# A two-layer trunk kernel: the second layer's first four tiles in pairs, features outermost, with a software-pipelined norm

## The chip, the cores and the metric

The kernel runs on one core of a Trainium2 chip. The metric is the device time of one execution in microseconds (us); lower is better. The engines named below are PE (TensorE, matmuls), DVE (VectorE), ACT (ScalarE), POOL (GpSimd) and SP (SyncE, which issues the DMAs). Each engine takes its instructions in the order in which the program was written for it; semaphores hold an instruction until its inputs are there.

## What is computed

Two layers of a trunk with four parallel branches, for 128 context tokens and 512 latent tokens (640 columns in all), with a model width of 1024. Cut to what matters here:

```python
def trunk_layer(x, cond, lp, ctx=None):
    mod = jax.nn.silu(cond) @ lp['w_mod'] + lp['b_mod']
    shift, scale, gate = jnp.split(mod[:, None, :], 3, axis=-1)
    h = rmsnorm(x, lp['g_norm']) * (1 + scale) + shift
    (a_u, a_v, b_r, b_k, b_v, b_wd, b_ad, c_q, c_k, c_v, d_p, z, mg) = split_in(h @ lp['w_in'])
    y_a = chunk_mix(a_u, a_v, ...)
    y_c = attention(c_q, c_k, c_v, ...)
    y_b, s_fin = rwkv7_mix(b_r, b_k, b_v, b_wd, b_ad, ...)
    y_d = pool_mix(d_p, ...)
    ys = jnp.stack([y_a, y_b, y_c, y_d], axis=2) * jax.nn.silu(z)
    up = jnp.einsum('blnc,ncd->blnd', ys, lp['w_up'])
    merged = jnp.sum(jax.nn.sigmoid(mg) * up, axis=2)
    return x + gate * (merged @ lp['w_o'])
```

The product `h @ w_in` is made tile by tile of 128 output columns. Its first four tiles are the keys, the values and the two query tiles of the attention: c_k, c_v, and two halves of c_q.

## The kernel before

**Layout.** Activations lie with features on the 128 partitions: the width of 1024 is eight blocks of features (`KT` = 8), and the 640 tokens are two halves `b` of 320 columns (`hs`, `segs`). The first half holds all context tokens, which have a modulation of their own, so a normed feature has two segments there and one in the second half.

**Products.** Every float32 product is made of three passes in a reduced format. Weight and activation are each split into a high and a low part, and `accum` (line 450) issues, for each feature block, hi x hi, hi x lo and lo x hi into one PSUM tile. The weights come in pieces of half a tile (four feature blocks). `piece()` hands out the next one in the order of the list `pieces`, and `split` makes the high part on ACT (`whi`) and the low part on DVE (`wlo`), by default two pieces ahead. `whi` and `wlo` have three buffers each, so a piece's buffers come free when the piece three before it has been used. The four PSUM tiles `m` take the products of the tiles, and `evac` copies them out on ACT and DVE in turn.

**The norm.** `normed` (line 603) takes the sum of squares through a matmul, a square root on ACT and a reciprocal on DVE. Then for each feature block: `t` = x times the modulation's scale times the norm's factor on DVE, `hi` = t + shift on ACT (rounded to the reduced format), and `lo` = t + shift - hi on DVE. With `ahead` set, `lo` of a block is issued behind `t` of the next one; without it, right after `hi`. In the first layer both halves go through it together with `ahead`; in the second layer each half has a call of its own, as soon as the last layer's output projection of that half is done, with `ahead` = 0.

**The order of work.** A planner in the kernel (class `Clock`) runs while the program is written. The main line is a generator whose matmuls fill PE; side jobs (norms, modulation, attention, scan, pooling) are generators too, and the planner steps each of them when, by its own reckoning, its inputs are ready. `yield VQ` lets a job rest until DVE's queue is nearly empty. What comes out is a fixed order of instructions for each engine.

**The head of the second layer.** `head` (line 1276) makes the tiles `HEAD` = ck, cv, q0, q1 for the first half of tokens while the second half's norm runs, and then for the second half. Each tile takes its eight feature blocks one after the other, waits for block k of the norm (`yield f"h{l}{b}.{k}"`), and is copied out by `put`, which marks the tile as ready after the second half. The weights of these tiles lie in SBUF already (`resident`, filled by `hold_wo`) and are split anew for each half of tokens. `attention` waits for the norm, then for ck, cv and q0, and rotates the keys and queries (`rotate`: a shuffle, two products, one of them on POOL, and a sum). q1 is rotated by a job of its own. Scores, softmax and values then run as side jobs. After the head the main line makes nine more tiles (wa, k0, v0, r0, k1, r1, v1, and the two gates z20 and z21), and `gated(None, ...)` needs the attention's result before it goes on. The scan of the second branch runs beside all this.

Of the kernel before, what the change touches and what calls it, by code (L numbers as in the profile page):

```python
# [17 lines left out]
KT = D // P  # L18
# [7 lines left out]
PASSES = (2, 0, 3, 1)  # L26

HEAD = ["ck", "cv", "q0", "q1"]
ORDER = ["wa", "k0", "v0", "r0", "k1", "r1", "v1", "z20", "z21", "p0", "av0", "p1", "av1", "au0", "au1", 0,
         "z00", "z01", 1, "z30", "z31", 2, "z10", "z11", 3]  # L30
A_TILES = HEAD + [n for n in ORDER if isinstance(n, str)]
A_INDEX = {n: i for i, n in enumerate(A_TILES)}
# [262 lines left out]
def hybrid_layers_kernel(ctx: ExitStack, tc: tile.TileContext, xt, cond, condb, wm, wt, wa, wb, wo, pa, pb, pc, gfin, kctx, vctx,  # L295
# [10 lines left out]
    def S(shape, tag, bufs=1, dt=F32):  # L306
        return ck.alloc(tag, sb.tile(shape, dt, tag=tag, name=tag, bufs=bufs), bufs)

    def M():
        return ck.alloc("m", ps_m.tile([P, HF], F32, tag="m", name="m"), 4)  # L310
# [10 lines left out]
    ck = Clock()  # L321
    V, A, G, PE = Engine(nc.vector, "V", ck), Engine(nc.scalar, "A", ck), Engine(nc.gpsimd, "G", ck), nc.tensor

    def dma(out, in_, wait=False, scale=4):
        ck.dma(out, in_, scale * out.size(), wait)
        nc.sync.dma_start(out, in_)
# [42 lines left out]
    pieces = []  # L369
    for l in range(NL):  # L370
        def a_piece(n, h):
            pieces.append((wa[l, A_INDEX[n]][:, 4 * P * h:4 * P * h + 4 * P], 4))

        if l == 0:
            for group in (HEAD[0:3], HEAD[3:4]):
                for h in range(2):
                    for n in group:
                        a_piece(n, h)
        else:
            for n in HEAD * 2:  # L380
                for h in range(2):
                    pieces.append(((l, n, h), 4))
        for it in ORDER:
            if isinstance(it, int):
                for d in range(KT):
                    for h in range(2):
                        pieces.append((wb[l, it, d][:, 5 * P * h:5 * P * h + 5 * P], 5))
            else:
                for h in range(2):
                    a_piece(it, h)  # L390
        for b in range(2):
            for d in range(KT):
                for h in range(2):
                    pieces.append(((l, d, h), 4))
    raws, splits, resident, x_first = {}, {}, {}, {}
    nxt = [0, 0, 0]
# [47 lines left out]
    def piece(ahead=2):  # L444
        i = nxt[2]
        nxt[2] += 1
        split(i + ahead)
        return splits.pop(i)
# [193 lines left out]
    def ksl(tl):  # L642
        return lambda k: tl[:, k]
# [8 lines left out]
    def layer(l, h, prb):  # L652
        rhs_h = []
# [622 lines left out]
        def head():  # L1276
            inputs["cv"] = S([P, T], "bon")
            at = None

            def put(n, b, o):  # L1280
                nonlocal at
                if at is None:
                    at = S([P, 2560], "xm0")
                    inputs["ck"] = at[:, 0:T]
                    inputs["kc"] = at[:, T:T + 256]
                    dma(inputs["kc"], kctx[l])
                    for f in range(2):
                        inputs[f"q{f}"] = at[:, T * (f + 1) + 256:T * (f + 2) + 256]
                evac(target(n, b), o)
                if b:  # L1290
                    ck.mark(L + n)

            ck.spawn(f"{L}at", attention(), 0)
            if l == 0:
                for b in range(2):
                    yield f"hh{l}{b}"
                rhs_h.extend((ksl(h[b][0]), ksl(h[b][1])) for b in range(2))
                out = [[M(), M()], [M(), M()], [CB()[:, 0:HF], OB()[:, 0:HF]]]
                ws = [piece(2 - i) for i in range(3)]
                for k in range(KT):  # L1300
                    turn = k % 4 == 3
                    for b, i in [(b, i) for i in range(3) for b in range(2)] if turn else [
                            (b, i) for b in range(2) for i in range(3)]:
                        yield f"h{l}{b}.{k}"
                        yield from accum([out[i][b]], ws[i], k % 4, 1, [rhs_h[b]], k, k == 0, k == KT - 1)
                        if turn and b:
                            if k + 1 < KT:
                                ws[i] = piece(0)
                            else:
                                split(nxt[2] + i)  # L1310
                yield f"n{l}0"
                for i in range(3):
                    for b in range(2):
                        put(HEAD[i], b, out[i][b])
                o = yield from main()
                for b in range(2):
                    put(HEAD[3], b, o[b])
            else:
                for b in range(2):
                    yield f"hh{l}{b}"  # L1320
                    rhs_h.append((ksl(h[b][0]), ksl(h[b][1])))
                    for n in HEAD:
                        o = M()
                        for hf in range(2):
                            w = piece()
                            for k in range(4):
                                yield f"h{l}{b}.{4 * hf + k}"
                                yield from accum([o], w, k, 1, [rhs_h[b]], 4 * hf + k, hf == 0 and k == 0,
                                                 hf == 1 and k == 3)
                        yield f"n{l}0"  # L1330
                        put(n, b, o)
        def scans(ta, k0, v0, kx):
            yield f"{L}atp"
            yield f"{L}wa"
            yield from scan(0, ta, k0, ta[:, 2], v0)
            yield from scan(1, S([P, 4, T], "A0"), kx[:, 0], kx[:, 1], kx[:, 2])
# [89 lines left out]
    def program():  # L1426
        xs, accs = [], []
        pbs = [S([P, NPB], "pb")]

        def x_half(b):  # L1430
            xh = x_tile(b)
            for k in range(0, KT, 4):
                dma(xh[:, k:k + 4], xt[:, b, k:k + 4])
            xs.append(xh)

        def params():
            dma(c_sb[:, CST_1:], cst[:, CST_1:])
            dma(pbs[0], pb[0])
            dma(gf, gfin)

        x_half(0)
        x_half(1)
        mod_tiles(0)
        mod = modulation([(0, n) for n in range(KT)], {1: lambda: load(2), KT: params})
        next(mod)
        for b in range(2):
            acc = S([P, HF], "nacc", 2)
            if b == 0:
                for k in range(KT):
                    sq_add(acc, xs[b][:, k], k == 0)  # L1450
            else:
                odd = S([P, 2, T], "yb")[:, 0, 0:HF]
                for k in range(KT):
                    sq_add(odd if k % 2 else acc, xs[b][:, k], k < 2, G if k % 2 else V)
                V.tensor_tensor(acc, acc, odd, ALU.add)
            accs.append(acc)
        for b in range(2):
            rstd_of(accs[b])
        split(1)
        end, ck.end = ck.end, ck.t  # L1460
        ck.spawn("mods0", mod, 0, ("x", 1))
        ck.end = end
        h = {}
        ck.spawn("n00", normed(xs, accs, 0, h, range(2), 1), 0, None)
        ck.spawn("rows", modulation_rows(), 3, None)
        for l in range(NL):
            if l:
                pbs.append(S([P, NPB], "pb"))
                dma(pbs[l], pb[l])
            mhl, sm = yield from layer(l, h, pbs[l])  # L1470
            h, xs = {}, []
            for b in range(2):
                acc = S([P, HF], "nacc", 2)
                xh, sq = yield from out_proj(l, b, mhl, acc, sm, xs)
                if l + 1 < NL:
                    dma(x_next[l][:, b], xh)
                    ck.spawn(f"n{l + 1}{b}", normed({b: xh}, {b: acc}, l + 1, h, [b], 0, sq), 0, None)
                else:
                    def fin(xh=xh, acc=acc, sq=sq, b=b):
                        rs = rstd_of(acc, sq)  # L1480
                        A.activation(xh[:, KT - 1], xh[:, KT - 1], AF.Copy, scale=gf[:, KT - 1:KT])
                        yield
                        for k in range(KT):
                            E = G if k in (1, 3, 6) else V
                            E.tensor_tensor(xh[:, k], xh[:, k], rs, ALU.mult)
                            if k % 2:
                                dma(y_o[:, b, k - 1:k + 1], xh[:, k - 1:k + 1])
                    ck.spawn(f"f{b}", fin(), 0)

    ck.run(program())  # L1490


# [132 lines left out]
```

## Time and profile before

| | us |
|---|---|
| median of 3 runs | 1424.76 |
| lowest and highest | 1424.6 to 1425.26 |
| the profiled execution | 1419.62 |
| its span on the core | 1417.8 |
| PE matmuls busy | 1355.5 (96%) |
| DVE busy | 946.1 (67%) |
| ACT busy | 567.3 (40%) |
| mean granted clock of PE | 0.988 |

Times inside the program count from the start of the span. A row of a timeline gives the start, the duration, the engine, the line of the code and the operation, what it writes and what it reads, and, in brackets, how long the engine had been idle before it and what released it. Most work goes through helpers, so the line is that of a helper (L289 for DVE and ACT, L330 for matmuls), and the tiles' names tell what it is. [...]

### The profile page before, as it was taken

The page shows a single profiled execution, that of the slowest core. Times are in us where ns is not written, and L with a number is a line of the kernel's source. Part 1 is how long each engine was busy: PE and PEld are TensorE (multiplying, and loading weights), DVE is VectorE, ACT ScalarE, POOL GpSimd, SP SyncE. Part 2 cuts the span into 40 slices and gives each one's busy share as a digit, 9 for nine tenths or more (in the row PEclk, how much of TensorE's full clock was granted, in tenths as well). Part 3 has the DMA queues.
Part 4 walks back from the last instruction along what each step waited for, and adds up shares of the span by engine and source line. Part 5 has one row for each costly group of instructions (what it writes and reads, how often), then busy time and mean ns, then how long its engine had stood idle before and what let it go on. Part 6 is the DMA issues. An engine that isn't in the chain of part 4 may idle for free.

```text
span 1417.8 us, 27575 instructions
## 1 busy us (share of the span) xinstructions
PE 1355.5 (96%) x11274; PEld 1254.9 (89%) x11274; DVE 946.1 (67%) x2096; ACT 567.3 (40%) x1252; POOL 50.1 (4%) x43
## 2 busy tenths in 40 slices
PE   5899989999999999999989998999999999999996
PEld 3788878988999989999979887898899999899996
DVE  7667678755777757558886667795466585464476
ACT  5455622235522333325444554223445233233363
POOL 0100000000000000000001000000000000000011
PEclk9999999999999999999999999999999999999998
DMA  9411114421223422751213111423112323134011
GB/s 372 144 53 61 68 48 116 118 70 55 81 79 103 120 71 66 241 203 63 74 61 114 58 56 50 116 74 103 40 54 70 93 80 87 39 131 169 28 38 74
DMA packets 86502, 132.59 MB, mean 94 GB/s; under 512 B 44744, under 2 KB 46152, under 8 KB 84456
## 3 DMA queue, kind: packets, MB, share of 16 engines
q1 hardware_dynamic: 86376, 130.84, 29.1%
q8 instruction: 88, 1.44, 0.4%
q14 instruction: 38, 0.31, 0.1%
HBM read 120.46 MB, written 10.35 MB: 92 GB/s over the span
## 4 chain that ended last, share of the span: by engine, by line
PE 84%; DVE 9%; ACT 4%; issue 2%; DMA 1%; SPq 0%; DVEq 0%; ACTq 0%
PE m L330 67%; PE x L330 9%; PE c L330 4%; PE o L330 2%; DVE wlo L289 2%; DVE t L289 2%; PE x L334 1%; DVE nacc L289 1%; DVE kb L289 1%; DVE lo L289 1%; ACT A L289 1%; PE o L334 1%; ACT vn L289 1%; DVE xm L289 1%; ACT whi L289 1%
## 5 line engine op out<-in xcount | busy, mean ns | idle before, releaser
L330 PE MATMUL m<-hi,whi 128*128 128x320 f32 x2064 | 668.4, 324 | 5.5 <-ACT hi L289 3.6
L330 PE MATMUL m<-lo,whi 128*128 128x320 f32 x2064 | 641.9, 311 | 4.6 <-DVE lo L289 3.8
L330 PE MATMUL m<-hi,wlo 128*128 128x320 f32 x2064 | 641.8, 311 | 2.5 <-DVE wlo L289 2.5
L330 PEld LDWEIGHTS m<-hi,whi 128*128 128x128 f32 x2064 | 391.0, 189 | 31.2 <-issue 12.0
L330 PEld LDWEIGHTS m<-lo,whi 128*128 128x128 f32 x2064 | 391.1, 189 | 9.6 <-DVE lo L289 6.1
L330 PEld LDWEIGHTS m<-hi,wlo 128*128 128x128 f32 x2064 | 390.6, 189 | 5.7 <-DVE wlo L289 5.4
L289 ACT CAST whi<-raw 128x640 fp32r<-128x640 f32 (+1 forms) x220 | 148.5, 681 | 282.1 <-PE m L330 264.2
L289 DVE TENSOR_TENSOR wlo<-raw,whi 128x640 fp32r<-128x640 f32 (+1 forms) x220 | 167.7, 765 | 112.8 <-ACT whi L289 110.4
L289 ACT ACTIVATE t<-m 128x320 f32<-128x320 f32 x160 | 68.0, 436 | 87.6 <-PE m L330 87.5
L289 DVE SCALAR_TENSOR_TENSOR t<-t,m 128x320 f32<-128x320 f32 x128 | 61.6, 481 | 57.9 <-PE m L330 42.8
L289 DVE TENSOR_TENSOR kb<-kb 80x31 f32<-80x31 f32 (+15 forms) x248 | 88.7, 358 | 12.5 <-DMA kb<-ad 5.7
L330 PE MATMUL m<-ysh,whi 128*128 128x320 f32 x256 | 83.5, 326 | 1.8 <-DVE t L289 1.6
L289 DVE CUSTOM_DVE_ANT_0 junk<-wt,sil 128x1024 bf16<-128x1024 f32 x64 | 78.1, 1220 | 4.9 <-DMA wt<-wt 4.8
L330 PE MATMUL m<-ysh,wlo 128*128 128x320 f32 x256 | 79.1, 309 | 0.0
L330 PE MATMUL m<-ysl,whi 128*128 128x320 f32 x256 | 79.0, 309 | 0.0
L330 PEld LDWEIGHTS m<-ysh,whi 128*128 128x128 f32 x256 | 48.0, 188 | 5.1 <-DVE t L289 2.1
L289 DVE TENSOR_TENSOR xm<-xm,t 128x320 f32<-128x320 f32 x96 | 48.5, 506 | 3.3
L289 DVE RECIPROCAL t<-t 128x320 f32<-128x320 f32 x16 | 34.4, 2149 | 21.3 <-ACT t L289 21.3
L330 PEld LDWEIGHTS m<-ysl,whi 128*128 128x128 f32 x256 | 48.1, 188 | 0.4
L330 PEld LDWEIGHTS m<-ysh,wlo 128*128 128x128 f32 x256 | 48.1, 188 | 0.0
L289 ACT ACTIVATE vn<-c 64x128 f32<-64x128 f32 x40 | 10.8, 271 | 80.8 <-DVE vn L289 80.8
L289 DVE CUSTOM_DVE_ANT_0 kbt<-x,xm 128x256 f32<-128x256 f32 (+2 forms) x72 | 28.6, 434 | 14.8 <-PE x L330 14.7
(234 smaller groups left out, 1519.6 us busy)
## 6 DMA issues: line engine op xcount, KB each, us to landing
raw<-wb SPq DMA_DIRECT2D x128, 320.0 KB, 2.8
raw<-wa SPq DMA_DIRECT2D x92, 256.0 KB, 2.7
wt<-wt SPq DMA_DIRECT2D x32, 512.0 KB, 3.7
A<-wm SPq DMA_DIRECT2D x4, 1024.0 KB, 9.0
A<-wo SPq DMA_DIRECT2D x8, 512.0 KB, 3.7
xm<-xt SPq DMA_DIRECT2D x4, 640.0 KB
ad<-A SPq DMA_DIRECT2D x8, 320.0 KB, 3.8
qr<-wm SPq DMA_DIRECT2D x2, 1024.0 KB
```

Source lines behind the costliest of these rows:

```text
L289: return f(out, *a, **k)
L330: PE.matmul(out, lhsT, rhs, start=start, stop=stop)
L334: PE.transpose(out, in_, K("ident"))
```

## The change

In the second layer, the second half of tokens is walked in two pairs of tiles, ck with cv and q0 with q1 (`PAIRS`). Within a pair the feature blocks are outermost: block k of the norm is multiplied into both tiles before block k+1 is waited for. The list of pieces follows: for this half it goes pair by pair, first halves of both tiles, then second halves. Three pieces are split at the start of each half pair, and the fourth when the first tile of the pair is through with its first half. The first half of tokens is walked as before. The norm of the second half is called with `ahead` = 1 (`b` takes the place of 0), that of the first half stays as it was.

```diff
@@ pieces
         else:
-            for n in HEAD * 2:
+            for n in HEAD:
                 for h in range(2):
                     pieces.append(((l, n, h), 4))
+            for pair in PAIRS:
+                for h in range(2):
+                    for n in pair:
+                        pieces.append(((l, n, h), 4))
@@ head
                 for b in range(2):
                     yield f"hh{l}{b}"
                     rhs_h.append((ksl(h[b][0]), ksl(h[b][1])))
+                    if b:
+                        break
                     for n in HEAD:
...
+                for pair in PAIRS:
+                    out = [M(), M()]
+                    for k in range(KT):
+                        if k % 4 == 0:
+                            ws = [piece(2), piece(1)]
+                        yield f"h{l}1.{k}"
+                        for i in range(2):
+                            yield from accum([out[i]], ws[i], k % 4, 1, [rhs_h[1]], k, k == 0, k == KT - 1)
+                            if k % 4 == 3 and i == 0:
+                                split(nxt[2] + 1)
+                    for i, n in enumerate(pair):
+                        put(n, 1, out[i])
@@ program
-                    ck.spawn(f"n{l + 1}{b}", normed({b: xh}, {b: acc}, l + 1, h, [b], 0, sq), 0, None)
+                    ck.spawn(f"n{l + 1}{b}", normed({b: xh}, {b: acc}, l + 1, h, [b], b, sq), 0, None)
```

## Rows read from the trace of the kernel before

**Rows 1.** Windows of the head: stretch, length, each engine's busy time, clock, DMA.

```profile
737.60:746.70 9.10, 5.38 (x14) 3.06 (x14) 6.58 (x13) 2.75 (x5) 0.00 (x0) 0.71 0.08 26
746.70:758.40 11.70, 11.70 (x78) 11.69 (x78) 7.86 (x17) 5.02 (x10) 1.66 (x1) 0.93 0.46 158
```

**Rows 2.** Timeline of PE over the head: start, duration, operation, idle time before.

```profile
739.82 0.42 PE L330 MATMUL m<-hi,whi 128*128 128x320 f32 x1 [2.09 <-ACT hi L289]
...
748.27 0.31 PE L330 MATMUL m<-hi,whi 128*128 128x320 f32 x1
...
758.36 0.31 PE L330 MATMUL m<-hi,wlo 128*128 128x320 f32 x1
```

**Rows 3.** Timeline of DVE over the second half's norm.

```profile
727.38 0.55 DVE L289 SCALAR_TENSOR_TENSOR lo<-t,shift,hi 128x320 fp32r<-128x320 f32 x1 [0.63 <-ACT hi L289]
728.21 1.29 DVE L289 TENSOR_TENSOR wlo<-kx,whi 128x512 fp32r<-128x512 f32 x2 [0.28 <-ACT whi L289]
729.42 0.48 DVE L289 COPY bon<-m 128x320 f32<-128x320 f32 x1
729.82 0.68 DVE L289 TENSOR_TENSOR wlo<-vn,whi 128x512 fp32r<-128x512 f32 x1
...
743.73 0.55 DVE L289 SCALAR_TENSOR_TENSOR lo<-t,shift,hi 128x320 fp32r<-128x320 f32 x1 [0.63 <-ACT hi L289]
744.20 0.55 DVE L289 SCALAR_TENSOR_TENSOR t<-xm,gsc,nacc 128x320 f32<-128x320 f32 x1
745.38 0.55 DVE L289 SCALAR_TENSOR_TENSOR lo<-t,shift,hi 128x320 fp32r<-128x320 f32 x1 [0.63 <-ACT hi L289]
```

**Rows 4.** Timeline of ACT over the head.

```profile
726.78 0.56 ACT L289 ACTIVATE hi<-t,shift 128x320 fp32r<-128x320 f32 x1 [2.81 <-DVE t L289]
727.25 0.41 ACT L289 COPY xm<-m 128x320 f32<-128x320 f32 x1
727.55 1.14 ACT L289 CAST whi<-kx 128x512 fp32r<-128x512 f32 x2
...
754.63 0.43 ACT L289 COPY xm<-m 128x320 f32<-128x320 f32 x1 [1.29 <-PE m L330]
```

**Rows 5.** Timeline of PE around the wait for the attention.

```profile
866.92 0.31 PE L330 MATMUL m<-hi,wlo 128*128 128x320 f32 x1
...
873.84 1.85 PE L330 MATMUL x<-bon,cst 128*128 128x320 f32 x4 [3.42 <-DVE bon L289]
```

**Rows 6.** Timeline of ACT: the attention's last copy.

```profile
870.47 0.27 ACT L289 COPY y<-o 128x128 f32<-128x128 f32 x1 [1.43 <-PE o L330]
```

**Rows 7.** Timeline of DVE: the rotations and first scores, and the first gated product.

```profile
758.31 0.73 DVE L289 STREAM_SHUFFLE vn<-xm 128x512 f32<-128x512 f32 x1
...
760.96 0.69 DVE L289 TENSOR_TENSOR xm<-xm,vn 128x512 f32<-128x512 f32 x1 [1.19 <-POOL xm L289]
...
761.64 0.48 DVE L289 COPY xm<-m 128x320 f32<-128x320 f32 x1
...
764.00 0.28 DVE L289 CUSTOM_DVE_ANT_0 kbt<-x,xm 128x128 f32<-128x128 f32 x1
...
765.43 0.73 DVE L289 STREAM_SHUFFLE vn<-xm 128x512 f32<-128x512 f32 x1
...
873.70 0.48 DVE L289 SCALAR_TENSOR_TENSOR t<-t,m 128x320 f32<-128x320 f32 x1
```

**Rows 8.** Windows of PE alone: length, busy time, clock, DMA share, GB/s.

```profile
22.00:24.00 2.00, 1.10 (x16) 1.00 1.02 341
...
872.00:874.00 2.00, 0.16 (x1) 1.00 0.12 28
874.00:876.00 2.00, 2.00 (x6) 0.63 0.00 0
```

**Rows 9.** Windows of PE in both layers, without heads and tails.

```profile
70.00:690.00 620.00, 607.45 (x5176) 0.99 0.30 94
760.00:1340.00 580.00, 569.91 (x4926) 0.99 0.27 79
```

More of the change, by code (lines that the diff above doesn't have):

```diff
@@ L28 @@
 HEAD = ["ck", "cv", "q0", "q1"]
+PAIRS = (HEAD[0:2], HEAD[2:4])
 ORDER = ["wa", "k0", "v0", "r0", "k1", "r1", "v1", "z20", "z21", "p0", "av0", "p1", "av1", "au0", "au1", 0,
```

## Prediction

> **What bounds the kernel now.** I read the page's busy shares first: the matmul engine (PE) is busy nearly all the time, so the change can pay only where PE stands still, or where its clock is low. The change touches one place, the first four tiles of the second layer (ck, cv, q0, q1; "the head" below), so I read that stretch alone: the windows, then the timelines of PE, VectorE (DVE) and ScalarE (ACT) beside each other. In 9.1 us from 737.6 PE is busy 5.4 us at a mean clock of 0.71, and the next stretch still has 0.93 [rows 1]. PE has walked the first four features of ck for the second half of the tokens and then waits 2.09 us for the next feature's hi part [rows 2]. This norm is therefore what ends last: its last lo starts at 745.38 and ends at 745.93 [rows 3]. From there PE runs without a gap to the last matmul of q1 at 758.36 [rows 2].
>
> Why the norm is slow is seen on DVE: of each feature it computes t, then waits 0.63 us for ACT's hi, then computes lo [rows 3]. Where nothing else is queued between, a feature costs 1.65 us (from the lo at 743.73 to the one at 745.38): twice 0.47 of DVE's time, and 0.7 of waiting and handing over.
>
> The third place to look is where the head's work ends up. The tiles feed the attention, which runs beside the main line, and the main line needs its result before the first gated product. The last matmul of the main line before that point starts at 866.92 [rows 5]. The attention's last copy is at 870.47 [rows 6]. The first step of the gated product on DVE follows at 873.70 [rows 7], because the scan's work stands ahead of it there; PE had waited 3.42 us up to 873.84 [rows 5]. So the main line arrives some 3 us early at this point: a head that is shorter for the main line alone only waits longer there.
>
> **The change, part by part.**
>
> *Pipelined norm.* On DVE, feature k's lo moves behind feature k+1's t. The count of instructions stays: 8 t, 8 hi, 8 lo. The wait of 0.63 us is filled by a lo, which takes 0.47 of it. But eight weight halves are also split in this stretch: ACT casts the high part (whi), DVE subtracts it (wlo). ACT takes its queue in order: in the rows, the casts of two halves at 727.55 stand behind the hi of 726.78, which had itself waited 2.81 us for t [rows 4]. With the lo moved, t of the next feature is queued earlier, and its hi stands in front of the next cast. Then wlo can start only 1.71 us after the start of t: 0.58 to hi (t's 0.55 and a handover), 0.47 from hi to what stands behind it (726.78 to 727.25), and 0.66 from a cast to its wlo (727.55 to 728.21) [rows 3, 4]. Of these DVE fills 0.47 with t and 0.47 with one lo; 0.77 is left as a wait. [...]
>
> Bounds: if DVE never waited after its first t, 16 norm steps at 0.47, nine wlo at 0.60 (two from 728.21 to 729.42) and two copies at 0.40 [rows 3] make 13.7 us, and from the first t at 726.2 (0.58 ahead of its hi) the norm would end at 739.9, 6 us earlier. With 0.77 us ahead of six of the wlo, 4.6 in all, and 1.5 us ahead of the first (from 726.7 to 728.21, with no lo to fill it) it ends at 746.0. I take the second, no gain, since each of these waits follows from the queue's order: a feature with a split behind it cost 1.65 + 0.60 = 2.25 us before, and costs 0.47 + 0.47 + 0.77 + 0.60 = 2.3 after; the last three features, which had no split between them, get three. The other end stays for the range.
>
> *Features outermost in pairs.* The same 96 matmuls per half of tokens run; two tiles now take each feature when it comes. At 745.93 the old order has 74 matmuls left. The new one has at most 9 of the pair ck/cv (the last feature and what waits of the one before) and 48 of q0/q1, 57 in all. One step is 0.147 us (65 steps from 748.27 to 758.36, less 0.5 for five transposes among them) [rows 2]. The old rest took 758.5 - 745.93 = 12.6 us: 10.9 of steps, 0.5 of transposes, and about 1.2 for the first eight at the lower clock (the window to 758.4 has 0.93 [rows 1]).
>
> *A tighter split.* The three buffers of split weights now serve two tiles at once, so the fourth half of a pair is cast only when the first tile has left its first half, 6 matmuls (0.88 us) before it is needed; before, a half was split two halves (24 matmuls) ahead. Cast to end of wlo takes 728.21 - 727.55 + 0.68 = 1.34 us [rows 3, 4]. That is a new wait of about 0.5 us at each half, of which the norm hides the one inside ck/cv; two remain, 1.0 us. If a rotation (3.3 us on DVE, from the shuffle at 758.31 to the end of the sum at 761.65 [rows 7]) comes ahead of such a wlo, the wait is up to 3 us more; I take none, since the halves are asked for before the marks that release a rotation.
>
> New rest: 57 x 0.147 + 0.5 + 1.0 = 9.9 us, so the head ends at 755.8 instead of 758.5: **2.7 us** for the main line. SP's queue: the weights of the head lie in SBUF, and the first load of wa still goes out three pieces ahead of its split, now at the end of ck/cv; that is half a pair (24 steps, 3.5 us) before the split and a whole one before its use. I cost the DMAs at nothing; without that cover a late load would hold wa by as much as it is late. POOL has nothing here but its product in each rotation, which moves with it.
>
> *What the attention gets.* Tile ck is finished at the same time as before, for it ends with the norm. cv is ready 4 us earlier, and is not what the attention waits for last. q0, copied at 754.63 before [rows 4], is now ready with q1 at the end of the head, about 755.8 to 756.2. Its rotation on DVE started at 758.31, 3.7 us after the copy; the same delay would make it 1.2 us later, no delay 2.1 us earlier. q1's copy was at 761.64 and its rotation at 765.43, between the first block's scores (764.00) and the rest of that block [rows 7]; it can now follow q0's at 759.6, up to 5.8 us earlier. The ends are therefore +1.2 and -5.8; I take **-2**, the bound of q0, on which the first scores wait.
>
> **How it sums.** At the wait near 867 the later of two counts: the main line arrives 2.7 us earlier, the attention 2 us earlier, so 2.0 us remain. After that point PE is bound by its own matmuls. In the profiled run (1419.62, of which the span is 1417.8) this makes 1417.6; the median of the runs shown is 5.14 above that execution, and moves likewise: 1424.76 - 2.0 = **1422.8**.
>
> **The rivals.**
> 1. *The attention does not follow.* Its start keeps the 3.7 us after the copy, or the shared wait at 867 swallows all: gain 0 to 1, 1424.2. For it: the norm and ck end when they did. A version of it is the clock: six matmuls (0.88 us) per feature of 2.3 us keep PE 40% busy over the end of the norm. PE fell to the lower clock after a stretch of 0.16 in 2 us (872 to 874), and kept the full one at 1.10 in 2 us [rows 8], so this lies between. A fall costs about 1.2 us, as now, which leaves 1.5 of the 2.7 for the main line. Chance 0.20 in all. [...]
> 2. *More is given back.* The norm ends earlier, between 739.9 and 745.9, and q1's early rotation takes 3.3 us out of the attention's first blocks: 4 to 7 us, middle 1419.5. For it: two rotations and the whole pair stand ready together. Against: ACT's order. Chance 0.22.
> 3. *Slower.* Where q0 and q1 are ready at once, both rotations are queued ahead of the first scores: 756.2 + 2 x 3.3 + the 2.4 us from rotation to first scores gives 765.2, 1.2 after the 764.00 of before. If the order of the rest, which is dealt anew by the planner, then puts one further block of DVE work of that size (3.3 us) ahead of the attention's end at 870, as the scan's steps stand there now, PE waits as much longer: +3.3, 1428.0. It decides once the attention's end lies over 2 us later than 870.5. The two layers, dealt differently, idle on PE 12.6 us in 620 and 10.1 us in 580 outside the heads and tails [rows 9], which shows 2 to 3 us as the size of such chance. Chance 0.19.
>
> **How the numbers follow.** Forecast 0.39 (1421.0 to 1424.3), rivals 0.20, 0.22, 0.19. A measurement can tell about 0.2% (2.85 us) from no change. Faster by more: rival 2 and 0.11 of the forecast, 0.33. Slower by more: 0.17 of rival 3 and 0.01 of rival 1, 0.18. Within: the rest, 0.49. The range reaches from 1.5 below the middle of rival 2 to just short of rival 3's price, 1418.0 to 1427.5, and leaves out a third of the one and half of the other.
>
> **What would show it.** In the changed profile: the last lo of this norm within 1 us of 745.9; PE steps of six matmuls between its waits; the last matmul of q1 near 755.8; waits of about 0.5 us for wlo at the pair's borders; the first scores near 762; and a wait before the first gated product near 867 that is not shorter. It is wrong if the norm ends before 743, if PE's clock stays low into q0/q1, or if the time after the head moves by more than the head.

## The result

The changed kernel is faster: a median of 1413.7 us (4 runs, 1411.22 to 1418.08) against 1424.68 us of the kernel before, a ratio of 0.9928 (95% interval 0.9911 to 0.9944). A second measurement of the same program gave 0.9932 (0.9912 to 0.9952). The gain is about 10 us, where 2 had been forecast and a range down to 1418.0 been given.

The two profiled executions hide this: 1418.08 us after, 1419.62 before. They differ in the first layer, where both programs issue the same instructions in the same order; yet the first t of the second half's norm in the second layer is at 733.56 us after and was at 726.2 before. So all stages below are counted from that t (called t0), which both programs reach with the same work done. From t0 to the end of the span it is 682.4 us after and 691.6 before, 9.2 us less.

| from t0 (us) | before | after | gained in the stage |
|---|---|---|---|
| last lo of the norm ends | 19.7 | 19.6 | |
| last matmul of q1, one step (0.15) after its start | 32.3 | 29.5 | 2.8 |
| first scores on DVE | 37.8 | 40.0 | |
| attention's last copy starts | 144.3 | 136.7 | |
| first gated product is cast | 148.5 | 142.3 | 3.4 |
| second gated product is cast | 329.9 | 320.4 | 3.3 |
| end | 691.6 | 682.4 | -0.3 |

"Gained in the stage" is what the difference grew by since the figure above it in that column. Where PE gained it behind the head is seen in its windows from q1 to the first and from there to the second gated product, in the kernel before and then in the changed one (length, busy time, clock as a share of full speed, DMA):

```profile
758.50:874.70 116.20, 111.38 (x861) 1.00 0.19 62
874.70:1056.10 181.40, 178.06 (x1698) 0.98 0.27 77
```

```profile
763.10:875.80 112.70, 110.99 (x860) 1.00 0.19 59
875.80:1053.90 178.10, 174.95 (x1698) 1.00 0.29 81
```

Up to the first gated product the matmuls take nearly the same time, and PE stands still for 1.7 us instead of 4.8. From there to the second one it stands still for as long as before, but the same 1698 matmuls take 175.0 us instead of 178.1. That is the clock: before, it fell behind the wait at the first gated product [rows 8] (0.50 from 874.70 to 877.70) and once more later in this stretch (the window below, 0.57); after, it kept the full level (1.00).

```profile
1021.00:1025.00 4.00, 4.00 (x15) 0.57 0.01 4
```

Now the head. These are PE's waits in it after the change (timeline of PE, as [rows 2]), with the last matmul of q1 at the end:

```profile
735.59 0.42 PE L331 MATMUL m<-hi,whi 128*128 128x320 f32 x1 [0.86 <-ACT whi L290]
736.32 0.41 PE L331 MATMUL m<-hi,wlo 128*128 128x320 f32 x1 [0.17 <-DVE wlo L290]
744.13 0.41 PE L331 MATMUL m<-hi,wlo 128*128 128x320 f32 x1 [0.17 <-DVE wlo L290]
749.32 0.42 PE L331 MATMUL m<-hi,wlo 128*128 128x320 f32 x1 [0.17 <-DVE wlo L290]
750.24 0.42 PE L331 MATMUL m<-lo,whi 128*128 128x320 f32 x1 [0.36 <-DVE lo L290]
752.53 0.42 PE L331 MATMUL m<-lo,whi 128*128 128x320 f32 x1 [1.15 <-DVE lo L290]
755.32 0.42 PE L331 MATMUL m<-hi,wlo 128*128 128x320 f32 x1 [0.17 <-DVE wlo L290]
760.19 0.42 PE L331 MATMUL m<-hi,wlo 128*128 128x320 f32 x1 [0.54 <-DVE wlo L290]
...
762.93 0.31 PE L331 MATMUL m<-hi,wlo 128*128 128x320 f32 x1
```

No single wait is over 1.15 us, where one of 2.09 stood before [rows 2]. The two waits of 0.17 and 0.54 us for a wlo at 755.32 and 760.19 are those of the tighter split. In the windows of the same stretches after t0 as in [rows 1] the clock is 1.00 in both, against 0.71 and 0.93.

```profile
744.97:754.07 9.10, 7.33 (x42) 6.02 (x42) 7.30 (x14) 3.93 (x8) 0.00 (x0) 1.00 0.10 26
754.07:765.77 11.70, 10.99 (x75) 10.46 (x74) 8.57 (x20) 4.67 (x10) 1.66 (x1) 1.00 0.55 175
```

The norm itself, in the timeline of DVE, as [rows 3]:

```profile
733.56 0.55 DVE L290 SCALAR_TENSOR_TENSOR t<-xm,gsc,nacc 128x320 f32<-128x320 f32 x1
735.57 1.29 DVE L290 TENSOR_TENSOR wlo<-kx,whi 128x512 fp32r<-128x512 f32 x2 [1.46 <-ACT whi L290]
736.78 0.55 DVE L290 SCALAR_TENSOR_TENSOR t<-xm,gsc,nacc 128x320 f32<-128x320 f32 x1
737.25 0.55 DVE L290 SCALAR_TENSOR_TENSOR lo<-t,shift,hi 128x320 fp32r<-128x320 f32 x1
...
748.57 0.69 DVE L290 TENSOR_TENSOR wlo<-y,whi 128x512 fp32r<-128x512 f32 x1 [0.67 <-ACT whi L290]
749.18 0.55 DVE L290 SCALAR_TENSOR_TENSOR t<-xm,gsc,nacc 128x320 f32<-128x320 f32 x1
749.64 0.54 DVE L290 SCALAR_TENSOR_TENSOR lo<-t,shift,hi 128x320 fp32r<-128x320 f32 x1
750.86 0.69 DVE L290 TENSOR_TENSOR wlo<-kx,whi 128x512 fp32r<-128x512 f32 x1 [0.68 <-ACT whi L290]
...
752.65 0.55 DVE L290 SCALAR_TENSOR_TENSOR lo<-t,shift,hi 128x320 fp32r<-128x320 f32 x1 [0.17 <-ACT hi L290]
```

No lo waits 0.63 us for its hi any more, but now wlo waits for its cast, 0.67 us in these rows (0.27 to 1.00 over all of them), and the first one 1.46 us. The cast's place is plain on ACT (as [rows 4]): the hi waits 1.22 us for t, and the cast stands right behind it.

```profile
749.76 0.56 ACT L290 ACTIVATE hi<-t,shift 128x320 fp32r<-128x320 f32 x1 [1.22 <-DVE t L290]
750.23 0.60 ACT L290 CAST whi<-kx 128x512 fp32r<-128x512 f32 x1
```

After the head, the rotations, the first scores and the first gated step on DVE (as [rows 7]):

```profile
766.19 0.74 DVE L290 STREAM_SHUFFLE vn<-xm 128x512 f32<-128x512 f32 x1
...
770.26 0.74 DVE L290 STREAM_SHUFFLE vn<-xm 128x512 f32<-128x512 f32 x1
...
773.52 0.28 DVE L290 CUSTOM_DVE_ANT_0 kbt<-x,xm 128x128 f32<-128x128 f32 x1
...
874.78 0.48 DVE L290 SCALAR_TENSOR_TENSOR t<-t,m 128x320 f32<-128x320 f32 x1
```

Both rotations now stand ahead of the first scores, which come 2.2 us later after t0 than before. At the other end of the attention, ACT and then PE (as [rows 6] and [rows 5]):

```profile
870.23 0.27 ACT L290 COPY y<-o 128x128 f32<-128x128 f32 x1 [2.20 <-PE o L331]
```

```profile
873.60 0.31 PE L331 MATMUL m<-hi,wlo 128*128 128x320 f32 x1
874.92 1.34 PE L331 MATMUL x<-bon,cst 128*128 128x320 f32 x4 [1.01 <-DVE bon L290]
...
877.25 0.41 PE L331 MATMUL m<-hi,whi 128*128 128x320 f32 x1 [0.56 <-DVE t L290]
```

The attention takes 96.7 us from first scores to last copy, against 106.5 before. It is over at 870.23, while the main line still works up to 873.60; PE then waits 1.01 and 0.56 us, where it had waited 3.42 us with a fall of the clock behind it (0.63) [rows 5, 8]. So the main line no longer waits for the attention.

The lead of the attention is not made at its start. It has ten blocks of scores. From t0, the eighth block's are at 106.6 us before and 97.0 after, the ninth's at 112.6 and 111.6, the tenth's at 132.6 and 120.2. In the timeline of DVE these are, before and then after:

```profile
832.81 0.41 DVE L289 CUSTOM_DVE_ANT_0 kbt<-x,xm 128x256 f32<-128x256 f32 x1
...
838.80 0.42 DVE L289 CUSTOM_DVE_ANT_0 kbt<-x,xm 128x256 f32<-128x256 f32 x1
...
858.83 0.42 DVE L289 CUSTOM_DVE_ANT_0 kbt<-x,xm 128x256 f32<-128x256 f32 x1 [3.57 <-PE x L330]
```

```profile
830.59 0.42 DVE L290 CUSTOM_DVE_ANT_0 kbt<-x,xm 128x256 f32<-128x256 f32 x1
...
845.17 0.42 DVE L290 CUSTOM_DVE_ANT_0 kbt<-x,xm 128x256 f32<-128x256 f32 x1
...
853.77 0.42 DVE L290 CUSTOM_DVE_ANT_0 kbt<-x,xm 128x256 f32<-128x256 f32 x1 [1.11 <-PE x L331]
```

So the lead comes and goes with the places that the planner gave to the blocks among the other jobs. The question of the experiments is what of this belongs to the change.

### The profile page after: what moved, and what is told of

The parts are those of the page before. It is cut to its first block, busy times and chain, and to the rows that moved or that the text cites. A ratio compares the mean times of both kernels' runs of the same rounds, so it can differ in the third digit from the quotient of the medians.

```text
span 1416.0 us, 27587 instructions
## 1 busy us (share of the span) xinstructions
PE 1358.9 (96%) x11274; PEld 1256.8 (89%) x11274; DVE 944.7 (67%) x2096; ACT 566.8 (40%) x1252; POOL 50.8 (4%) x43
## 3 DMA queue, kind: packets, MB, share of 16 engines
q1 hardware_dynamic: 86376, 130.84, 30.1%
## 4 chain that ended last, share of the span: by engine, by line
PE 81%; DVE 10%; ACT 4%; issue 2%; DMA 2%; SPq 0%; POOL 0%; DVEq 0%; ACTq 0%; POOLq 0%
PE m L331 63%; PE x L331 10%; PE c L331 4%; PE o L331 2%; DVE wlo L290 2%; DVE t L290 2%; DVE kb L290 2%; ACT whi L290 1%; DMA kb<-ad 1%; PE x L335 1%; DVE nacc L290 1%; PE o L335 1%; DVE lo L290 1%; ACT vn L290 1%; ACT A L290 1%
## 5 line engine op out<-in xcount | busy, mean ns | idle before, releaser
L331 PEld LDWEIGHTS m<-lo,whi 128*128 128x128 f32 x2064 | 390.1, 189 | 10.2 <-DVE lo L290 7.1
L290 ACT CAST whi<-raw 128x640 fp32r<-128x640 f32 (+1 forms) x220 | 148.7, 682 | 296.3 <-PE m L331 270.6
```

Source lines behind the costliest of these rows:

```text
L290: return f(out, *a, **k)
L331: PE.matmul(out, lhsT, rhs, start=start, stop=stop)
```

## The experiments

In the table, "first gated" is the first cast of the gated product, "end" the end of the span, both in us from t0; the ratio is that of the whole time to the kernel before. The edits follow below.

| | last lo ends | first scores | attention's last copy | first gated | end | ratio (95% interval) |
|---|---|---|---|---|---|---|
| before, first profile | 19.7 | 37.8 | 144.3 | 148.5 | 691.6 | 1 |
| before, second profile (e10) | 19.7 | 38.8 | 145.3 | 149.5 | 691.9 | 0.9992 (0.9974 to 1.0009) |
| e2, norm pipelined only | 18.3 | 36.2 | 151.1 | 155.1 | 690.0 | 0.9984 (0.9968 to 0.9999) |
| e4, before, longer head | 19.7 | 41.8 | 148.3 | 152.6 | 695.4 | 1.0027 (1.0012 to 1.0042) |
| e5, before, planner -2.5 | 19.7 | 39.2 | 142.9 | 145.5 | 691.3 | 0.9992 (0.9980 to 1.0005) |
| e11, before, planner -1.2 | 19.8 | 39.3 | 148.1 | 151.6 | 697.8 | 1.0056 (1.0035 to 1.0076) |
| e7, before, planner +2.5 | 19.7 | 41.8 | 146.6 | 148.8 | 697.7 | 1.0040 (1.0024 to 1.0055) |
| e13, before, scan's keys late | 19.7 | 38.9 | 144.6 | 146.2 | 694.5 | 1.0018 (0.9996 to 1.0040) |
| e16, before, rotations first | 19.7 | 42.8 | 144.3 | 146.9 | 692.6 | 0.9996 (0.9979 to 1.0013) |
| after, first profile | 19.6 | 40.0 | 136.7 | 142.3 | 682.4 | 0.9928 (0.9911 to 0.9944) |
| after, second profile (e9) | 19.6 | 40.9 | 137.6 | 143.2 | 683.4 | 0.9932 (0.9912 to 0.9952) |
| e1, pairs only | 20.3 | 40.5 | 137.2 | 142.8 | 681.8 | 0.9933 (0.9911 to 0.9956) |
| e3, after, longer head | 19.6 | 41.8 | 138.5 | 144.1 | 683.8 | 0.9948 (0.9929 to 0.9966) |
| e6, after, planner +2.5 | 19.7 | 39.4 | 140.6 | 146.6 | 687.2 | 0.9972 (0.9958 to 0.9986) |
| e12, after, planner +1.2 | 19.6 | 40.0 | 141.5 | 145.0 | 689.1 | 0.9983 (0.9964 to 1.0001) |
| e8, after, planner -2.5 | 19.7 | 41.8 | 152.2 | 155.6 | 689.9 | 0.9983 (0.9966 to 1.0000) |
| e14, after, scan's keys late | 19.6 | 40.7 | 137.4 | 139.9 | 692.6 | 1.0004 (0.9985 to 1.0024) |
| e15, after, keys late in both layers | 19.6 | 41.9 | 138.8 | 141.2 | 693.0 | 1.0039 (1.0023 to 1.0056) |
| e17, after, q1's rotation later | 19.6 | 36.7 | 145.2 | 148.7 | 695.4 | 1.0024 (1.0008 to 1.0040) |

The times from t0 are those of one profile each, the ratios those of 4 to 12 runs. Apart from e15, whose first layer is edited too, the two agree within 2 us.

### Which half of the change: e1 and e2

e1 is the changed kernel with `normed(..., [b], 0, sq)` again. 

> The changed kernel with the second half's norm as before (lo right behind hi); only the walk in pairs is left. Theory A (the pairs shorten the head by about 2.5 us, the moved lo gives nothing; the rest of the gain is the order after the head): the last q1 matmul ends 2 to 3 us earlier after the norm's first t than in the kernel before, the norm's length stays within 0.7 us of 19.7 us, and the whole time is anywhere from 8 us less to 3 us more, since the order after the head is dealt anew. Theory B (the moved lo carries the gain): within 2 us of the kernel before. Theory C (the head's gain is swallowed at the wait for the attention): within 2 us of the kernel before with a head that is 2 to 3 us shorter.

e2 is the kernel before with `normed(..., [b], b, sq)`, and the old walk. 

> The kernel before with the second half's norm pipelined (lo behind the next t) and the old walk, tile by tile. Theory A: the head's length within 1 us of the kernel before (32.3 us from the norm's first t to the end of q1), since the norm ends no earlier; whole time within what a new order gives, 4 us either way. Theory B: 5 us or more shorter, most of it in the head.

The pairs alone give all of it: 681.8 us, ratio 0.9933, more than the 8 us that theory A had allowed. Their norm ends at 20.3 us, 0.7 later than with the moved lo, and the last matmul of q1 0.5 us later (30.1 after t0). The moved lo alone makes the norm 1.5 us shorter in the old walk, where no half is split between the last three features, though theory A had it end no earlier; the head gets 0.5 us shorter (31.8), and the whole time hardly (0.9984). Theories B and C fall. In e1's timeline of DVE the old rhythm is back, t, a wait of 0.63, lo:

```profile
743.22 0.54 DVE L290 SCALAR_TENSOR_TENSOR t<-xm,gsc,nacc 128x320 f32<-128x320 f32 x1
744.39 0.55 DVE L290 SCALAR_TENSOR_TENSOR lo<-t,shift,hi 128x320 fp32r<-128x320 f32 x1 [0.63 <-ACT hi L290]
744.86 0.54 DVE L290 SCALAR_TENSOR_TENSOR t<-xm,gsc,nacc 128x320 f32<-128x320 f32 x1
```

### Does the head's length pass on to the end: e3 and e4

Both have 18 more matmuls of which the planner knows nothing, so that the order of all else stays. Their product is overwritten by the first real one.

```diff
 # e3 (changed kernel), ahead of the pair q0/q1
+if k == 0 and pair is PAIRS[1]:
+    for _ in range(18):
+        PE.matmul(out[0], ws[0][0][:, 0], rhs_h[1][0](0), start=True, stop=True)
 # e4 (kernel before), ahead of q0 in the second half
+if b and hf == 0 and n == "q0":
+    for _ in range(18):
+        PE.matmul(o, w[0][:, 0], rhs_h[b][0](0), start=True, stop=True)
```

> The changed kernel with 18 more matmuls on PE (2.65 us) ahead of the pair q0/q1, unknown to the planner, so the order of everything else is that of the changed kernel. Theory A (the main line's time in the head passes on to the end): 2 to 3 us slower than the changed kernel's 0.9928 of before, so about 0.9945. Theory C (swallowed at the wait for the attention): within 0.7 us of the changed kernel. Theory D (the head alone makes the gain of 11 us): 5 us or more slower than the changed kernel.

> The kernel before with the same 18 more matmuls ahead of q0's second half, order otherwise unchanged. Theory A: 2 to 3 us slower than before. Theory C: within 0.7 us of before, for the main line arrives early at the wait near 867 us anyway. Theory D: 5 us or more slower.

On PE they are one line of e4, 2.80 us long:

```profile
754.10 2.80 PE L1328 MATMUL m<-hi,whi 128*128 128x320 f32 x18
```

In e4 the first scores, the attention's last copy and the first gated product are each 4.0 us later than in the first profile of the kernel before, the end 3.8; against the second profile, whose clock in the 32 us from t0 was that of e4 (0.84 in both), it is 3.0 and 3.5. In e3 they are 1.8 us later and the end 1.4, against the first profile of the changed kernel. So a delay of main line and attention together goes through to the end within half a us, as long as the order stands: the wait at the first gated product ("the gate") swallows nothing that also delays the attention. Theory C falls. So does theory D: e3's head is 31.4 us long, only 1.0 less than the old one, and yet 683.8 us remain of 691.6. The order, not the length of the head, carries most of the gain.

### Other orders of the same work: e5 to e8, e11, e12, with e9 and e10

One line after the head moves the planner's clock. No instruction is added and none is delayed; the side jobs and the main line are only interleaved otherwise from there on.

```diff
         yield from head()
+        if l:
+            ck.t += -2.5      # e5 and e8; +2.5 in e6 and e7; -1.2 in e11; +1.2 in e12
         yield f"mods{l}"
```

> The kernel before, head and all, but the planner's clock is set 2.5 us back at the end of the second layer's head, so that the order of what follows is dealt as if the head had been that much shorter. Nothing is computed differently and no engine is delayed. Theory A1 (6 us of the gain are the order after the head as it happens to fall): from the norm's first t to the end between 682 and 696 us, and over 2 us away from the 691.6 us of before. Theory A2 (the gain follows from the pairs as such): within 2 us of 691.6.

> The changed kernel with the planner's clock set 2.5 us ahead at the same place, so that what follows is ordered as if the head had its old length. Theory A1: over 2 us away from the changed kernel's 682.4 us from the norm's first t to the end, up to 692; the head's 2.8 us stay. Theory A2: within 2 us of 682.4.

> The kernel before with the planner's clock set 2.5 us ahead at the end of the head: another order of the rest with the same head. Theory A1: between 682 and 696 us from the norm's first t, with no relation to the sign of the shift. Theory A2: within 2 us of 691.6.

> The changed kernel with the planner's clock set 2.5 us back at the end of the head. Theory A1: between 680 and 692 us from the norm's first t. Theory A2: within 2 us of 682.4.

> The changed kernel as it is, for a second profile: how far the stages of one program repeat. Theory A1 (the order after the head makes some 6 us): from the norm's first t to the end 682.4 again within 1.5 us, head and wait at the gate as in the first profile. Theory A3 (the difference after the head is chance of the execution, clock falls above all, and not the order): 685 us or more, with other waits.

> The kernel before as it is, for a second profile. Theory A1: 691.6 us from the norm's first t to the end again within 1.5 us, with the wait at the gate and the fall of the clock behind it. Theory A3: 688 us or less, or 694 or more.

> The kernel before with the planner's clock set 1.2 us back at the end of the head: half the shift of the earlier run. Theory A1: another value between 682 and 698 us from the norm's first t to the end, not in line with 691.6 and 691.3 at shifts of 0 and -2.5. Theory A2 (the old walk as such costs the 9 us): 690 to 693.

> The changed kernel with the planner's clock set 1.2 us ahead at the end of the head. Theory A1: anywhere between 680 and 691 us. Theory A2: 681 to 684. Theory A4 (an order far from the one measured is worse, a near one as good): 682 to 685.

The second profiles settle A3: the same program comes back within 1.0 us (682.4 and 683.4; 691.6 and 691.9), so the difference after the head is not chance of an execution. The shifts speak against A2: with the same head as before, other orders end at 691.3, 697.8 and 697.7; with the pairs at 687.2, 689.1 and 689.9, where the changed kernel has 682.4. Sign and size of the shift do not order them. e5, which deals as if the head were 2.5 us shorter, gains nothing and ends as A2 had it. The expected lower end for the old walk (682) did not come; e11 was at its upper end, and e7 1.7 us beyond. A4 falls too: the near order (e12) is no better than the far ones. What such an order costs is seen around the gate: windows of PE (length, busy time, clock, DMA) of the changed kernel, and then of e8 with the same head.

```profile
860.00:880.00 20.00, 17.80 (x138) 1.00 0.16 48
880.00:900.00 20.00, 19.13 (x170) 1.00 0.30 92
```

```profile
860.00:880.00 20.00, 11.65 (x97) 0.83 0.16 48
880.00:900.00 20.00, 19.46 (x156) 1.00 0.22 65
```

In e8 PE is idle for 8 of the first 20 us, as the attention ends at 152.2 after t0 (876.6 in the span), and the clock falls there (0.83).

The second profile of the changed kernel shows one more thing: there the clock does fall in the head, 0.89 and 0.78 of full in these windows of PE, and the head with all that follows is 0.9 us later. In the 32 us from t0 the mean clock is 1.00 in seven of the ten profiles with the pairs and 0.95 in three (e9, e14, e15); in all nine with the old walk it is 0.84 or 0.89.

```profile
742.00:746.70 4.70, 3.01 (x14) 0.89 0.13 31
746.70:752.00 5.30, 5.30 (x32) 0.78 0.98 312
```

### Is it the wait at the gate: e13, e14, e15

The scan's steps that stand ahead of the first gated product in DVE's queue are released behind it, in the second layer (e13, e14) or in both layers (e15).

```diff
+                if d and ft == 0 and l == 1:      # e15: without "and l == 1"
+                    yield f"{L}gd"
                 yield from keys(d)
...
         g2 = yield from gated(None, f"{L}at")
+        ck.mark(f"{L}gd")
```

> The kernel before with one step of a side job moved: in the second layer the scan's keys of the second direction (the kb, qr and bon steps on DVE and the product that reads bon on PE) are released only after the first gated product, ahead of which they stood in DVE's and PE's queues. Theory A5 (the wait at the gate near t0 + 141 to 150 us, with the clock that falls behind it, is where most of the 6 us outside the head are lost): the steps of the gated product follow the attention's last copy within 1 us, no fall of the clock there, and 684 to 689 us from the norm's first t to the end instead of 691.6. Theory A6 (that wait is made good elsewhere, the loss lies in the sum of the order): 690 to 695.

> The changed kernel with the same step moved. Theory A5: within 2 us of the changed kernel's 682.4 to 683.4 us, for its wait there is already only 1.6 us. Theory A6: between 684 and 692, as any other order.

> The changed kernel with the same step moved in both layers; the first layer has a wait of 4.0 us for bon at the same place. Theory A5: the first layer is 4 to 6 us shorter (the norm's first t of the second layer at about 721 instead of 726 us), the whole time 0.989 to 0.990 of before. Theory A6: the first layer within 2 us of its old length.

A5 falls. The gate is indeed passed earlier (146.2 instead of 148.5 after t0 in e13, 139.9 instead of 142.3 in e14), but the end is 2.9 and 10.2 us later than in the first profiles, as A6 had it for e13 and 0.6 us beyond it in e14. The scan is a chain as well, and what it lost is waited for elsewhere: from the first to the second gated product PE stands still for 7.5 us in e13 and 8.8 in e14, instead of 3.3 and 3.2. In e14 much of it comes soon: the window after the gate, of PE, and a wait in it for a step y on DVE, ahead of which the moved steps now stand (qr and bon, 887.33 to 890.52):

```profile
880.00:900.00 20.00, 15.98 (x83) 0.83 0.13 40
```

```profile
891.64 0.47 PE L335 MATMUL x<-cst,xm 128*128 128x128 f32 x1 [3.42 <-DVE y L290]
```

e15 shows no gain in the first layer (t0 at 733.8 us, within the spread of 724.4 to 734.3 of all profiles). Behind the head it has e14's order and repeats its end (693.0 and 692.6), but its ratio is 1.0039 against 1.0004, so its first layer is rather some 5 us longer. A single wait, however plain in the profile, was not the place to mend.

### Is it the order of the rotations: e16 and e17

```diff
 # e16 (kernel before): scores held until q1 is ready, so that its rotation comes first
             rotate(q2[0], 1)
+            if l:
+                yield f"{L}q1"
 # e17 (changed kernel): q1's rotation held until the first block's scores are issued
                 yield f"{L}q1"
+                if l:
+                    yield f"{L}sc0"
                 rotate(q2[1], 0)
...
+                    if i == 0:
+                        ck.mark(f"{L}sc0")
```

> The kernel before with the attention's scores held until q1 is rotated too, so that both rotations stand ahead of the first scores, as they do in the changed kernel. Theory A7 (this order of rotations is what makes the attention 10 us shorter in the changed kernel): from the first scores to the attention's last copy 96 to 99 us instead of 106.5, and 683 to 687 us from the norm's first t to the end. Theory A1 (any change of order gives another value): between 689 and 698 us, as the other orders with the old walk.

> The changed kernel with q1's rotation held until the first block's scores are issued, as the kernel before has it. Theory A7: the attention takes 104 us or more from the first scores, and 687 to 691 us from the norm's first t to the end. Theory A1: between 681 and 693, as the other orders with the pairs.

Half of A7 came. The attention takes 101.5 us from first scores to last copy in e16 instead of 106.5, since the scores start 5.0 us later than in the first profile and it ends where it did; nothing is gained at the end (692.6). e17 loses 13 us against the changed kernel, more than A7 or A1 said and more than any other order with the pairs; its attention takes 108.5 us, though its first scores come 3.2 us earlier. Around the gate it looks like the orders above (windows of PE):

```profile
860.00:880.00 20.00, 13.52 (x97) 0.84 0.18 48
880.00:900.00 20.00, 19.66 (x135) 0.91 0.18 53
```

So the place of that rotation is not a cause that can be carried over by itself; each such move is a new order.

### What stays open

Six further orders of the old walk (e2, e5, e7, e11, e13, e16) end at 690.0 to 697.8 us, a mean of 694.0; six with the pairs (e1, e6, e8, e12, e14, which e15 repeats, and e17) at 681.8 to 695.4, a mean of 689.3. The difference is 4.7 us, and 2.8 of it can be the head; the spreads are too wide to say whether the pairs favour good orders beyond that. Nor is it shown that the good order is chance. e1 is no second draw: PE's order in it is that of the changed kernel until 155 us after t0, past the gate. And a planner whose clock is shifted may deal worse for that reason alone: with a clock left as it is and no job held back, the old walk ends at 691.6 and 690.0 (e2) and the pairs at 682.4 and 681.8 (e1), and no shift or hold was more than 0.3 us better than the kernel that it was made in. No run here tells these two readings apart. Which choices of the planner make the good order isn't settled either: moving one wait (e14) or one rotation (e17) destroyed it. No version here beat the changed kernel; e1, without the moved lo, equals it.

## Why the prediction was wrong

**The norm: right.** The forecast took no gain from the moved lo, with 0.77 us ahead of six of the wlo, 4.6 in all, and 1.5 us ahead of the first. The trace has 3.6 us in all, 0.27 to 1.00 each, and 1.46, and the norm ends 19.6 us after t0 against 19.7; that it fits so well is in part luck, for the rest of DVE's time came out 0.7 us longer than summed. e1 shows two parts that cancel: the walk in pairs makes the norm 0.6 us longer (20.3), and the moved lo makes it 0.7 shorter again.

**The head: right.** 2.7 us were forecast, 2.8 measured; behind the norm's last lo 55 matmuls are left where 57 were counted. The waits for the tighter split were given 0.5 us at each half, 1.0 in all, and are 0.17 and 0.54. No rotation was to come ahead of such a wlo, but one did: the sum of ck's rotation ended on DVE just ahead of the wlo behind the second wait, which stayed short all the same. The clock held in the first profile and fell in the second, which cost about 0.9 us, so the case left between two rows [rows 8] can go either way.

**The attention: wrong.** The step "I take **-2**, the bound of q0" failed twice. q0's rotation started 32.6 us after t0 instead of 32.1, no earlier: q0 was copied at 763.22, and DVE then made two splits, q1's copy and some small steps of the scan before the rotation at 766.19. And the first scores came 2.2 us later, as rival 3 had it (1.2 later, through both rotations). By e3 and e4, with a fixed order such a delay would have gone through to the end as a loss. But the attention then ran 9.8 us faster and ended 7.6 us earlier. The forecast had treated its length as given.

**The sum: wrong.** 2.0 us were forecast up to the gate; the gate is passed 6.2 us earlier, 2.8 by the head and 3.4 behind it, for PE stands still there for 1.7 us instead of 4.8. "After that point PE is bound by its own matmuls" put what follows at nothing and left out 3.3 us that were gained between the first and the second gated product: the matmuls are the same, but before the clock fell twice in that stretch and after it did not (0.98 of full speed became 1.00, 178.1 us of matmuls 175.0). And the planner's chance was mis-sized: 2 to 3 us were read from the idle time of the two layers [rows 9], but that is the difference of two sums in one program. Orders of the same work, measured, spread by 7.8 us with the old walk and by 13.6 with the pairs. Less 7.8, the forecast of 1422.8 would be 1415.0, and less 13.6 it would be 1409.2; only a range of the larger size takes in the 1413.7 that was measured.

**The rivals.** The second, "more is given back", was nearest: 4 to 7 us, by an attention that starts better. The amount was too small and the mechanism not as told, for the norm did not end earlier and the first scores came later. Of the first rival, the swallowing wait falls by e3 and e4; its other version, a loss of clock in the walk over waits, came half: PE kept the full clock in one of the changed kernel's two profiles (1.00) and lost 0.9 us in the other, while the tile-by-tile walk had 0.71 [rows 1]. In the 32 us from t0 no profile with the pairs had a lower clock than one with the old walk (0.95 and more against 0.89 and less).

## What to carry to other kernels

When a loop waits for a producer, give each arriving piece to two consumers; when the last piece lands, less is then left to do, even if the producer gets no faster (here 55 matmuls instead of 74, a tile being 24). Moving a step ahead on one engine (lo on DVE) gained little here, 0.7 us of a norm of 20.3: the step that it makes ready stands ahead of another's work on the next engine (the cast on ACT started right behind a hi that had waited 1.22 us). In a kernel whose order comes from a planner, an edit is measured together with a new order of all that follows: change only the order a few times, with the edit and without, before the gain is put down to the edit.

## What the runs showed that was not expected

The same instructions in the same order took 724.4 to 734.3 us up to t0 in the profiles of this study (e15 left aside, whose first layer is edited), a spread of 10 us in the first layer, while the stages behind t0 repeated within 1.0 us for either kernel. Stages are therefore better compared from a common landmark than from the start of the span.
